# Latent attention of a decoder block on one Trainium2 core: instructions placed by a list scheduler written into the kernel, softmax reciprocals on VectorE, more low parts on GpSimd

## The chip, the cores and the metric

The kernel runs on one core of a Trainium2 chip. The time is device microseconds of that core, from several runs of the same program; the median is used. One further execution was taken with the hardware profiler. The engines are TensorE (PE; PEld is its weight load), VectorE (DVE), ScalarE (ACT), GpSimd (POOL) and SyncE (SP), which only issues transfers here. The built program has one queue of instructions for each engine, in a fixed order, with waits for the other engines' work.

## The reference

One layer of a decoder block on 1024 positions of width 1024, float32:

```
h = rmsnorm(x);  proj = h @ w_in  -> q, k, v of sliding-window attention, q_lat, kv_lat, k_rope, two gates
o_a = sliding-window attention (8 heads, window 128, sinks)
qb = rmsnorm(q_lat) @ w_uq  (8 heads x 96),  kvb = rmsnorm(kv_lat) @ w_ukv
for each 128-query block:  s = (q_nope k_nope + q_rope k_rope) * scale, causal
                           p = softmax(s);  o_b = p @ v
y = sigmoid(g_a) * (o_a @ w_o_swa) + sigmoid(g_b) * (o_b @ w_o_mla)
x = x + y @ w_out
x = x + (silu(rmsnorm(x) @ w_gate) * (rmsnorm(x) @ w_up)) @ w_down
out = rmsnorm(x)
```

The change concerns the latent attention (`o_b`): 8 heads, each with 8 blocks of 128 queries against up to 1024 keys.

## The kernel before

Products of float32 precision are made of three fast matmuls. Each operand is split into a high part (a rounded copy, made by ScalarE: a CAST at line 160) and a low part (the difference, a TENSOR_TENSOR at line 161, usually on VectorE), and `mm3` (lines 167 to 169) adds high x high, high x low and low x high in one PSUM bank.

The stages follow one another: projections, sliding-window attention with the gates' products, latent attention, output mixing (`mix_a`, `mix_b`), the product with `w_out`, the feed-forward part, the last norm.

In latent attention a step is one head h and one query block n, in the order n = 2, 3, 6, 7, 0, 1, 4, 5, so that a tile is (n + 1) x 128 keys wide: 384, 512, 896, 1024, 128, 256, 640, 768. For each step:

- `scores(t)`: PE makes the scores (tile `scb`, lines 1134 to 1136) in one of two score buffers; VectorE adds the mask and takes the row maximum (line 1144, with a read of its accumulator into `nmb`); ScalarE takes the exponential with the row sum (line 1145, tile `p`), after which the score buffer is free; GpSimd inverts the row sum `denb` by a power of -1 (line 1146) and scales `p` (line 1147).
- `transposes(t)`: PE turns `p` in groups of up to four 128x128 blocks (line 1161, tile `pTb`), ScalarE and VectorE split each group into `pth` and `ptl`.
- `pv(h, j)`: after every second block, PE multiplies with the values into the bank `ob` (lines 1183 and 1184); ScalarE copies one half to `otb` (line 1189) and VectorE adds it to the other (line 1195).

Between them stand the products that prepare the next heads: `prod_q` (tile `q`, then `qf` at line 1084, then `qT`, whose low part is on GpSimd) and `prod_k` (tile `k`, then `kT`), the splitting of their weights (`wr` to `wuq`), and in the last heads the splitting of the sliding-window outputs (`oar` to `wv`), of this attention's outputs (`ob` to `obT`), of the mixing weights (`wr` to `wh` and `wl`) and seven early `mix_a` products (tile `oA`). The tiles `pTb`, `ob`, `q`, `k` and the early `oA` share four PSUM banks.

The code writes the steps in a loop over t, with the scores two steps ahead and the other pieces tied to step numbers by tables (`OA_LOAD`, `OA_SPLIT`, `early`). The earlier stages set the order of some engines by hand (`tc.manual_schedule`), but this one does not: the framework orders every engine's queue here, starting from the order of the code.

Of the kernel before, what the change touches and what calls it, by code (L numbers as in the profile page):

```python
# [8 lines left out]
F32 = mybir.dt.float32  # L9
# [8 lines left out]
P = 128  # L18
# [33 lines left out]
class Stream:  # L52
# [30 lines left out]
    def get(self, key):  # L83
        i = self.index[key]
        self.conv_to(i)
        return self.done.pop(i)


@with_exitstack
def hybrid_block_kernel(  # L90
# [1023 lines left out]
    live = {}  # L1114
    pts = {}
    po_live = {}

    order = [2, 3, 6, 7, 0, 1, 4, 5]

    def step(t):  # L1120
        return t // NB, order[t % NB]

    def scores(t):
        h, n = step(t)
        w = (n + 1) * P
        sc = PX("scb", (P, 1024))
        qh, ql = qT[h]
        kh, kl = kT[h % 3]
        cw = 320 if w == 640 else 512
        for c0 in range(0, w, cw):  # L1130
            c1 = min(c0 + cw, w)
            kc = slice(c0, c1)
            o = slice(c0 // cw * 512, c0 // cw * 512 + c1 - c0)
            nc.tensor.matmul(sc[:, o], qh[:, blk(n)], kh[:, kc], start=True, stop=False)
            nc.tensor.matmul(sc[:, o], qh[:, blk(n)], kl[:, kc], start=False, stop=False)
            nc.tensor.matmul(sc[:, o], ql[:, blk(n)], kh[:, kc], start=False, stop=True)  # L1136
        nm = tiny("nmb")
        p = U("p")
        den = tiny("denb")
        s_, m_, p_ = sc[:, 0:w], mask[:, S - w:], p[:, 0:w]  # L1140
        if cw == 320:
            s_ = sc.rearrange("p (a c) -> p a c", a=2)[:, :, 0:320]
            m_, p_ = (v.rearrange("p (a c) -> p a c", a=2) for v in (m_, p_))
        nc.vector.tensor_tensor_reduce(s_, s_, m_, 1.0, -NEG, op0=ALU.add, op1=ALU.min, accum_out=nm)  # L1144
        nc.scalar.activation(p_, s_, AF.Exp, scale=-1.0, bias=nm, accum_out=den)  # L1145
        nc.gpsimd.tensor_tensor(den, den, neg_one[:, 0:1], op=ALU.pow)  # L1146
        nc.gpsimd.tensor_scalar(p[:, 0:w], p[:, 0:w], den, 0.0, op0=ALU.mult, op1=ALU.add)  # L1147
        live[t] = p

    def transposes(t):  # L1150
        h, n = step(t)
        p = live.pop(t)
        j, odd = divmod(n, 2)
        if not odd:
            pts[(h, j)] = [(U("pth", F32R, (P, 4, 256)), U("ptl", F32R, (P, 4, 256)))
                           for _ in range((2 * j + 5) // 4)]
        for k0 in range(0, n + 1, 4):
            m = min(4, n + 1 - k0)
            pp = P1("pTb", (P, 4, P))
            for i in range(m):  # L1160
                nc.tensor.transpose(pp[:, i], p[:, blk(k0 + i)], ident)  # L1161
            hi, lo = pts[(h, j)][k0 // 4]
            split(hi[:, 0:m, blk(odd)], lo[:, 0:m, blk(odd)], pp[:, 0:m])

    def pv(h, j):
        tiles = pts.pop((h, j))
        js = []
        for q in order:
            if q % 2:
                js.append(q // 2)  # L1170
        i = js.index(j)
        first = i % 2 == 0
        pair = sorted(js[i // 2 * 2:i // 2 * 2 + 2])
        slot = pair.index(j)
        if first:
            po_live[h] = P1("ob", (P, 2, 256))
        po = po_live[h][:, slot]
        nk = 2 * j + 2
        for kb in range(nk):
            q_off = P if kb == nk - 1 else 0  # L1180
            hi, lo = tiles[kb // 4]
            vst = vM[kb][:, h]
            nc.tensor.matmul(po[:, q_off:], vst, hi[:, kb % 4, q_off:], start=kb == 0, stop=False)
            nc.tensor.matmul(po[:, q_off:], vst, lo[:, kb % 4, q_off:], start=False, stop=kb == nk - 1)
        if not first:
            po = po_live[h]
            tmp = U("otb")
            tv = tmp[0:64, 0:512].rearrange("p (a c) -> p a c", a=2)
            nc.scalar.copy(tv, po[64:128])
            if h % 2 == 0 and i == 1:  # L1190
                ob[h // 2] = U("ob")
            r = (h % 2) * 64
            ov = ob[h // 2][r:r + 64].rearrange("p (a c) -> p a c", a=4)
            ov = ov[:, pair[0]:pair[1] + 1:pair[1] - pair[0]]
            nc.vector.tensor_tensor(ov, po[0:64], tv, op=ALU.add)

# [7 lines left out]

    def split_oa(g, sh, c):
        raw, (hi, lo) = oa_raw[(g, sh)] if c == 0 else oa_raw.pop((g, sh))
        split(hi[:, c], lo[:, c], raw[:, c])
        oaT[(2 * g + c, sh)] = (hi[:, c], lo[:, c])
# [12 lines left out]
    def mix_a(dc, sh, ps):  # L1221
        if sh == 0:
            if dc < 4:
                ar[dc] = U("ar")
            if dc % 2 == 0:
                wo[dc // 2] = st.get(("oa", dc // 2))
        w = wo[dc // 2]
        mm3(ps, [((w[0][:, c, blk(dc % 2)], w[1][:, c, blk(dc % 2)]), oaT[(c, sh)]) for c in range(4)])
        if dc < 4:
            nc.scalar.copy(ar[dc][:, half(sh)], ps)  # L1230
        else:
            ga = gate[dc][:, half(sh)]
            nc.vector.tensor_tensor(ga, ps, ga, op=ALU.mult)
# [5 lines left out]
    def split_ob(c, sh):  # L1239
        if sh == 0:  # L1240
            ob_hl[c] = hi_lo("obT")
        hi, lo = ob_hl[c]
        src = ob.pop(c) if sh else ob[c]
        split(hi[:, half(sh)], lo[:, half(sh)], src[:, half(sh)])
        obT[(c, sh)] = (hi[:, half(sh)], lo[:, half(sh)])

    wo = {}
    OA_LOAD = {-26: (0, 0), -22: (1, 0), -14: (0, 1), -10: (1, 1)}
    OA_SPLIT = {-22: (0, 0, 0), -20: (0, 0, 1), -18: (1, 0, 0), -16: (1, 0, 1),
                -10: (0, 1, 0), -8: (0, 1, 1), -6: (1, 1, 0), -4: (1, 1, 1)}  # L1250
    NT = NH * NB
    psum_phase("psb", 2)
    scores(0)
    scores(1)
    early = {0: (0, 0), 1: (1, 0), 3: (0, 1), 4: (1, 1), 5: (2, 0), 6: (2, 1), 7: (3, 0)}
    pvq = []
    for t in range(NT):
        h, n = divmod(t, NB)
        if t + 2 < NT:
            scores(t + 2)  # L1260
        while pvq and pvq[0][0] <= t:
            pv(*pvq.pop(0)[1:])
        if n == 0 and h % 2 == 0 and h + 2 < NH:
            st.load_to(st.index[("uq", h // 2 + 1)])
        if n == 0 and h % 2 == 1 and h + 1 < NH:
            wuq[(h + 1) // 2] = st.get(("uq", (h + 1) // 2))
        if h + 1 < NH:
            if n in (2, 4):
                prod_q(h + 1, n // 2 - 1)
            if n in (3, 5) and h % 2 == 1:  # L1270
                prod_k((h + 1) // 2, n // 2 - 1)
# [598 lines left out]
```

## Time and profile before

| what | value |
|---|---|
| median of the runs | 1364.37 us (1363.83 to 1364.56, 3 runs) |
| the profiled execution | 1360.19 us, its span 1358.4 us |
| busy, share of the span | PE 98%, DVE 70%, ACT 48%, POOL 44% |
| granted TensorE clock | 0.999 |
| latent attention | from 370 to about 568 us |

A span is the time from the first to the last instruction of the profile. Busy times are sums of instruction durations; those of PE are modelled at their ends. A row of the timeline gives the start, the duration, the engine, the line, the operation, the tiles as output<-input with shapes, and in brackets how long the engine had been idle before and what released it. A row of the waits gives the waiting engine, tile and line, what it waited for, the total in us, the number of times and the longest. Groups by line give total busy us and mean ns.

### The profile page before, as it was taken

Reading aid. Unit: us, or ns where it says so; the run is one execution under the profiler, and the core shown is the slowest. Engines: PE = TensorE matmul, PEld = TensorE weight load, DVE = VectorE, ACT = ScalarE, POOL = GpSimd, SP = SyncE. Lnnn points to the kernel's source line nnn. Section 1 sums busy time; section 2 is a strip of 40 time slices with the busy share of each in tenths; the row PEclk is TensorE's granted clock in tenths of the full one; section 3 lists DMA queues with packets and bytes.
Section 4 is the critical chain, followed back from the end, with each engine's and each line's share of the span. In section 5 each row is a group of like instructions: output and inputs, shape, how many; then the busy total and the mean of one; then the engine's idle time right before and its main releaser. Section 6 shows DMA issues by size and latency. Waiting matters only on the chain.

```text
span 1358.4 us, 18967 instructions
## 1 busy us (share of the span) xinstructions
PE 1331.8 (98%) x6552; PEld 1112.0 (82%) x6552; DVE 944.6 (70%) x1527; ACT 653.4 (48%) x1317; POOL 596.2 (44%) x636
## 2 busy tenths in 40 slices
PE   9999999999999999999999999999999999999997
PEld 6899878878788888888887788888888888888886
DVE  6868767776777887489878866666656664664862
ACT  7433667665567777654357232322332332644452
POOL 1115545553066555131045875766665541022521
PEclk9999999999999999999999999999999999999999
DMA  9454332335100111598041353645444425996503
GB/s 360 161 182 154 115 106 82 98 121 174 71 2 13 43 32 32 219 307 264 31 171 62 112 188 140 227 178 178 147 153 165 163 85 184 379 385 237 171 16 140
DMA packets 78239, 205.39 MB, mean 151 GB/s; under 512 B 8768, under 2 KB 15424, under 8 KB 77504
## 3 DMA queue, kind: packets, MB, share of 16 engines
q1 hardware_dynamic: 76848, 199.99, 41.5%
q0 software_dynamic: 1152, 4.19, 1.6%
q8 instruction: 52, 0.85, 0.3%
q14 instruction: 43, 0.35, 0.1%
q10 hardware_dynamic: 144, 0.00, 0.0%
HBM read 141.24 MB, written 59.77 MB: 148 GB/s over the span
## 4 chain that ended last, share of the span: by engine, by line
PE 72%; DVE 7%; ACT 4%; issue 3%; POOL 3%; DMA 0%; POOLq 0%; ACTq 0%; DVEq 0%
PE fa L169 7%; PE fa L167 7%; PE fa L168 7%; PE fd L168 5%; PE fd L167 5%; PE fd L169 5%; PE fb L167 5%; PE fb L169 5%; PE fb L168 5%; DVE wl L161 2%; PE pTb L1161 2%; PE xo L167 1%; PE xo L168 1%; PE xo L169 1%; PE oA L167 1%
## 5 line engine op out<-in xcount | busy, mean ns | idle before, releaser
L161 DVE TENSOR_TENSOR wl<-wr,wl 128x512 fp32r<-128x512 f32 x150 | 154.6, 1052 | 75.4 <-ACT wl L160 75.1
L161 DVE TENSOR_TENSOR lrv<-lr,lrv 128x1024 fp32r<-128x1024 f32 x77 | 105.0, 1396 | 49.7 <-ACT lrv L160 47.1
L160 ACT CAST lrv<-lr 128x1024 fp32r<-128x1024 f32 x77 | 80.1, 1052 | 96.3 <-PE fd L169 56.0
L169 PE MATMUL fd<-lrv 128*128 128x512 f32 x308 | 119.9, 389 | 0.0
L168 PE MATMUL fd<-lrv 128*128 128x512 f32 x308 | 119.9, 389 | 0.0
L167 PE MATMUL fd<-lrv 128*128 128x512 f32 x308 | 119.9, 389 | 0.0
L172 POOL TENSOR_TENSOR wr<-wr,sm 128x512 f32<-128x512 f32 (+1 forms) x38 | 46.8, 1241 | 121.2 <-DVE wl L161 115.1
L160 ACT CAST wl<-wr 128x512 fp32r<-128x512 f32 x150 | 87.3, 623 | 3.1 <-DVE wr L816 2.6
L161 DVE TENSOR_TENSOR wl<-sm,wl 128x512 fp32r<-128x512 f32 x60 | 55.2, 946 | 45.4 <-ACT wl L160 45.4
L295 POOL TENSOR_SCALAR ms<-ss 128x1 f32<-128x1 f32 x32 | 9.8, 305 | 140.4 <-ACT xn L1582 62.5
L1146 POOL TENSOR_TENSOR denb<-denb,neg_one 128x1 f32<-128x1 f32 x64 | 36.4, 570 | 75.0 <-ACT p L1145 64.3
L167 PEld LDWEIGHTS fd<-lrv 128*128 128x128 f32 x308 | 57.8, 188 | 12.1
L169 PEld LDWEIGHTS fd<-lrv 128*128 128x128 f32 x308 | 57.8, 188 | 12.0
L168 PEld LDWEIGHTS fd<-lrv 128*128 128x128 f32 x308 | 57.8, 188 | 11.9
L1145 ACT ACTIVATE p<-scb,nmb 128x384 f32<-128x384 f32 (+3 forms) x64 | 47.5, 743 | 36.8 <-DVE nmb L1144 35.0
L161 DVE TENSOR_TENSOR ptl<-pTb,pth 128x512 fp32r<-128x512 f32 (+2 forms) x96 | 50.0, 549 | 13.6 <-ACT pth L160 12.8
L1144 DVE CUSTOM_DVE_ANT_0 scb<-scb,mask 128x384 f32<-128x384 f32 (+3 forms) x64 | 48.5, 758 | 14.1 <-PE scb L1136 13.7
L1485 ACT ACTIVATE act<-sm 128x512 f32<-128x512 f32 x11 | 7.0, 633 | 103.7 <-DVE sm L175 103.7
L1147 POOL TENSOR_SCALAR p<-p,denb 128x384 f32<-128x384 f32 (+3 forms) x64 | 49.1, 768 | 6.3
L1485 ACT ACTIVATE act<-pu 128x512 f32<-128x512 f32 x22 | 13.9, 632 | 74.8 <-DVE pu L175 74.8
L160 ACT CAST pth<-pTb 128x512 fp32r<-128x512 f32 (+2 forms) x96 | 42.9, 482 | 13.5 <-PE pTb L1161 12.9
L169 PE MATMUL fa<-t1h,wl 128*128 128x512 f32 x120 | 46.8, 391 | 2.6 <-DVE wl L161 2.6
(354 smaller groups left out, 4374.8 us busy)
## 6 DMA issues: line engine op xcount, KB each, us to landing
lr<-la_d SPq DMA_DIRECT2D x77, 256.0 KB, 5.4
wr<-in_w_gate_dram SPq DMA_DIRECT2D x22, 512.0 KB, 4.3
wr<-in_w_up_dram SPq DMA_DIRECT2D x22, 512.0 KB, 5.0
wd<-in_w_down_dram SPq DMA_DIRECT2D x22, 512.0 KB, 6.4
rb_d<-wd SPq DMA_DIRECT2D x22, 512.0 KB, 2.6
la_d<-sd SPq DMA_DIRECT2D x22, 512.0 KB, 4.8
lr<-rb_d SPq DMA_DIRECT2D x44, 256.0 KB, 5.4
lr<-in_w_down_dram SPq DMA_DIRECT2D x33, 256.0 KB, 5.6
```

The lines of the kernel that those rows point to most:

```text
L160: nc.scalar.copy(hi, src)
L161: (eng or nc.vector).tensor_tensor(lo, src, hi.bitcast(F32), op=ALU.subtract)
L167: nc.tensor.matmul(ps, ah, bh, start=first and i == 0, stop=False, skip_group_check=go_on)
L168: nc.tensor.matmul(ps, ah, bl, start=False, stop=False, skip_group_check=go_on)
L169: nc.tensor.matmul(ps, al, bh, start=False, stop=last and i == n - 1, skip_group_check=go_on)
L172: eng.tensor_tensor(out, a, b, op=ALU.subtract)
L1144: nc.vector.tensor_tensor_reduce(s_, s_, m_, 1.0, -NEG, op0=ALU.add, op1=ALU.min, accum_out=nm)
L1145: nc.scalar.activation(p_, s_, AF.Exp, scale=-1.0, bias=nm, accum_out=den)
L1146: nc.gpsimd.tensor_tensor(den, den, neg_one[:, 0:1], op=ALU.pow)
L1147: nc.gpsimd.tensor_scalar(p[:, 0:w], p[:, 0:w], den, 0.0, op0=ALU.mult, op1=ALU.add)
L1161: nc.tensor.transpose(pp[:, i], p[:, blk(k0 + i)], ident)
L1485: nc.scalar.activation(dst, src, AF.Silu)
```

## The change

The loop over steps is taken out. Each piece of work becomes a step of a `Plan` with an engine, an assumed duration in ns, the steps that it comes after, a rank, and the PSUM buffer that it takes or gives back: S (scores), M (maximum), E (exponential), W (reciprocal), C (scaling), T, H, L (transposes, high and low part), V, O, A (values, copy, sum), Q and K with their splits, u, o, w and b (splits of weights and outputs), G (early mixing products). `Plan.run` builds the order with a clock of its own: for each engine it takes, among the steps that could start within 30 ns of the earliest one, the step of lowest rank (its place in the sequence plus a constant for its kind), and issues the engine's earliest choice. PE, DVE, ACT and POOL then keep exactly this order in the stage; SP is left to the framework.

Two things change in what is computed where. The reciprocal of the row sum is a VectorE reciprocal in place of a GpSimd power. And the low parts of `wuq`, `wv` (from `oar`), `obT` and the four mixing weights converted here are made by GpSimd in place of VectorE; `qT` was there before. All 64 steps, all matmuls and all transfers remain; the splits of the last output block, which stood behind the loop, come into the plan, and so does the eighth early mixing product.

```diff
+    TAIL = {"E": 0, "D": 80, "A": 100, "P": 36, "S": 0}
+    HOP = {"E": 70, "D": 36, "A": 36, "P": 79, "S": 50}
+
...
+    def add(self, name, eng, cost, emit, after=(), rank=0.0, take=None, give=None, port=False, group=None):
+        self.steps[name] = (eng, cost, emit, list(after), rank, take, give, port, group)
+
...
+                for name in names:
+                    _, _, _, _, rank, take, _, _, group = steps[name]
+                    t = max(free[eng], since[name])
+                    if take is not None:
+                        s = slots[take[0]]
+                        if group in rows:
+                            if rows[group][turn[group]] != name:
+                                continue
+                            s = [s[turn[group] % len(s)]]
+                        if take[2] and sum(x < busy for x in s) <= take[2]:
+                            continue
+                        t = max(t, min(s) + self.HOP[eng])
+                    if t < busy:
+                        can.append((t, rank, name))
+                if can:
+                    t0 = min(can)[0]
+                    t, rank, name = min((c for c in can if c[0] <= t0 + self.slack), key=lambda c: (c[1], c[2]))
+                    if best is None or t < best[0]:
+                        best = (t, name)
+            t, name = best
+            eng, cost, emit, _, _, take, give, two, group = steps[name]
+            ready[eng].remove(name)
+            if eng == "P" or two:
+                t = max(t, port)
+                port = max(port, t + (100 if eng == "P" and not two else cost - 140))
+            end[name] = t + cost + (160 if eng == "E" else 0)
+            free[eng] = t + cost - self.TAIL[eng]
...
-        nc.vector.tensor_tensor_reduce(s_, s_, m_, 1.0, -NEG, op0=ALU.add, op1=ALU.min, accum_out=nm)
-        nc.scalar.activation(p_, s_, AF.Exp, scale=-1.0, bias=nm, accum_out=den)
-        nc.gpsimd.tensor_tensor(den, den, neg_one[:, 0:1], op=ALU.pow)
-        nc.gpsimd.tensor_scalar(p[:, 0:w], p[:, 0:w], den, 0.0, op0=ALU.mult, op1=ALU.add)
...
-        hh, nn = step(t)
-        if nn % 2 == 1:
-            pvq.append((t + 3, hh, nn // 2))
-        e = t - (NT - 8)
-        if e in OA_LOAD:
-            load_oa(*OA_LOAD[e])
-        if e in OA_SPLIT:
-            split_oa(*OA_SPLIT[e])
-        if e == -5:
-            st.conv_to(st.index[("oa", 0)])
-        if -3 <= e < 3:
-            split_ob((e + 3) // 2, (e + 3) % 2)
-        if e == 6:
-            psum_phase("psc", 4)
-        if e == 7:
-            st.conv_to(st.index[("ob", 0)])
-        if e in early:
-            mix_a(*early[e], (PX if e >= 6 else P1)("oA"))
-        if e == 4:
-            st.conv_to(st.index[("oa", 1)])
...
+    plan = Plan(30)
+    RANK = {'S': -2.38, 'M': -0.6, 'E': -2.86, 'W': -2, 'C': -2, 'V': 3.5, 'O': 1.49, 'A': 2.32, 'Q': -0.9, 'Qm': 2.11, 'Qh': 1.76, 'Ql': 0.5, 'K': -0.3, 'Kh': 0.92, 'Kl': 0.91, 'uh': -1.71, 'ul': -0.83, 'wl': 6.31, 'G': 2.93, 'wh': 0.76, 'bl': 0.9, 'ol': -0.89, 'H': -0.5, 'oh': -0.63}
+    LOW = {'Q': 'P', 'u': 'P', 'o': 'P', 'b': 'P', 'w': 'P'}
...
+        def maxes():
+            t_["p", key] = U("p")
+            nm = t_["nm", key] = tiny("nmb")
+            s_, m_, _ = views(t_["p", key])
+            nc.vector.tensor_tensor_reduce(s_, s_, m_, 1.0, -NEG, op0=ALU.add, op1=ALU.min, accum_out=nm)
+
+        def exps():
+            den = t_["den", key] = tiny("denb")
+            s_, _, p_ = views(t_["p", key])
+            nc.scalar.activation(p_, s_, AF.Exp, scale=-1.0, bias=t_.pop(("nm", key)), accum_out=den)
+            t_.pop(("sc", key))
+
+        def invert():
+            den = t_["den", key]
+            nc.vector.reciprocal(den, den)
+
+        def scale():
+            p, den = t_["p", key], t_.pop(("den", key))
+            nc.gpsimd.tensor_scalar(p[:, 0:w], p[:, 0:w], den, 0.0, op0=ALU.mult, op1=ALU.add)
+
...
+        add_step("M", *key, x=x, eng="D", emit=maxes, cost=210 + 1.055 * w, after=[("S", *key)])
+        add_step("E", *key, x=x, eng="A", emit=exps, cost=350 + 0.836 * w, after=[("M", *key)], give=("sc", key))
+        add_step("W", *key, x=x, eng="D", emit=invert, cost=100, after=[("E", *key)])
+        add_step("C", *key, x=x, eng="P", emit=scale, cost=232 + 0.878 * w, after=[("W", *key)], port=True)
...
+    def lower(kind, key, x, cost, hi, lo, src, after=()):
+        add_step(kind + "h", *key, x=x, eng="A", emit=lambda: nc.scalar.copy(hi(), src()), cost=cost[0], after=after)
+        on_p = LOW[kind] == "P"
+        add_step(kind + "l", *key, x=x, eng="P" if on_p else "D", port=True, cost=cost[1 + on_p], after=[(kind + "h", *key)],
+                 emit=lambda: sub(lo(), src(), hi().bitcast(F32), nc.gpsimd if on_p else nc.vector))
...
+        add_step("Q", h, s, x=x, eng="E", emit=prod, cost=2060, take=("p", ("q", h, s), 1),
+                 after=[("ul", h // 2, 0), ("ul", h // 2, 1), ("S", h - 2, NB - 1)])
+        add_step("Qm", h, s, x=x, eng="D", emit=rope, cost=683, after=[("Q", h, s)], give=("q", h, s))
+        lower("Q", (h, s), x, (621, 692, 1290), lambda: part(0), lambda: part(1), lambda: t_["qf", h, s],
+              [("Qm", h, s), ("S", h - 2, NB - 1)])
...
+    by_plan = tc.manual_schedule(engines={engines.PE, engines.DVE, engines.Activation, engines.Pool})
+    by_plan.__enter__()
+    plan.run({"x": 2, "p": 4, "w": 4}, {"S": [("S", h, i) for h in range(NH) for i in range(NB)]})
+    by_plan.__exit__(None, None, None)
...
-    split_ob(3, 0)
-    split_ob(3, 1)
+    ob.clear()
```

The order of the built programs differs at these places. The first is PE at the start of the stage, at the scores (`scb`) of the second tile and what follows. Before:

```order
L1134 MATMUL scb_4179<-kT_3994,qT_4037 128x512
L1135 MATMUL scb_4179<-kT_3994,qT_4037 128x512
L1136 MATMUL scb_4179<-kT_3994,qT_4037 128x512
L1134 MATMUL scb_4190<-kT_3994,qT_4037 128x512
L1135 MATMUL scb_4190<-kT_3994,qT_4037 128x512
L1136 MATMUL scb_4190<-kT_3994,qT_4037 128x512
L1134 MATMUL scb_4190<-kT_3994,qT_4037 128x384
```

Now:

```order
L1270 MATMUL scb_4174<-kT_3994,qT_4037 128x512
L1271 MATMUL scb_4174<-kT_3994,qT_4037 128x512
L1272 MATMUL scb_4174<-kT_3994,qT_4037 128x512
L256 MATMUL q_4183<-cq_3810,wuq_3916 128x512
L257 MATMUL q_4183<-cq_3810,wuq_3916 128x512
L258 MATMUL q_4183<-cq_3810,wuq_3916 128x512
L256 MATMUL q_4183<-cq_3811,wuq_3916 128x512
```

The third tile's scores (`scb_4190` before) now come nine matmuls later, behind a product `q` for the next head. The second place is ACT towards the end of head 6, at the exponential of the 640-wide tile. Before:

```order
L1145 ACTIVATE p_5966,denb_5967<-scb_5961,nmb_5965 128x256
L160 CAST pth_5946<-pTb_5985 128x4x128
L160 CAST wv_5809<-oar_5808 128x512
L160 CAST obT_6051<-ob_4394 128x512 x2
L160 CAST obT_6118<-ob_4947 128x512 x2
L160 CAST wh_5974<-wr_5972 128x1024
L160 CAST obT_6191<-ob_5510 128x512
L1145 ACTIVATE p_6000,denb_6001<-scb_5992,nmb_5999 128x640
L160 CAST obT_6191<-ob_5510 128x512
```

Now:

```order
L1290 ACTIVATE p_5984,denb_5988<-scb_5961,nmb_5985 128x256
L1326 CAST pth_5958<-pTb_5990 128x4x128
L1326 CAST pth_5976<-pTb_5997 128x4x128
L1376 CAST qT_5941<-qf_5995 128x512
L1326 CAST pth_6027<-pTb_6015 128x128
L1290 ACTIVATE p_6032,denb_6042<-scb_6004,nmb_6033 128x640
L1326 CAST pth_6027<-pTb_6044 128x2x128
L1290 ACTIVATE p_6047,denb_6069<-scb_6035,nmb_6048 128x768
L1357 COPY otb_6077<-ob_6018 64x512
L1326 CAST pth_6094<-pTb_6080 128x4x128
L1290 ACTIVATE p_6085,denb_6099<-scb_6072,nmb_6086 128x384
L1376 CAST obT_6112<-ob_4407 128x512
```

The conversions of `obT` and of the mixing weight `wh` stood in a row ahead of that exponential; now they stand later, one or two at a time between exponentials. The third place is POOL in head 4, at the scaling of the 1024-, 128- and 256-wide tiles. Before:

```order
L1146 TENSOR_TENSOR denb_5317<-denb_5317,neg_one 128x1
L1147 TENSOR_SCALAR p_5316<-p_5316,denb_5317 128x1024
L1146 TENSOR_TENSOR denb_5335<-denb_5335,neg_one 128x1
L1147 TENSOR_SCALAR p_5334<-p_5334,denb_5335 128x128
L161 TENSOR_TENSOR qT_5355<-qf_5366,qT_5355 128x512
L1146 TENSOR_TENSOR denb_5398<-denb_5398,neg_one 128x1
L1147 TENSOR_SCALAR p_5397<-p_5397,denb_5398 128x256
```

Now, from the 512-wide tile on:

```order
L1299 TENSOR_SCALAR p_5279<-p_5279,denb_5284 128x512
L261 TENSOR_TENSOR wv_5334<-oar_5197,wv_5334 128x512
L1299 TENSOR_SCALAR p_5300<-p_5300,denb_5312 128x896
L1299 TENSOR_SCALAR p_5319<-p_5319,denb_5339 128x1024
L1299 TENSOR_SCALAR p_5362<-p_5362,denb_5368 128x128
L261 TENSOR_TENSOR qT_5365<-qf_5347,qT_5365 128x512
L261 TENSOR_TENSOR wv_5334<-oar_5197,wv_5334 128x512
L1299 TENSOR_SCALAR p_5415<-p_5415,denb_5419 128x256
```

The powers are gone from this queue, and low parts of `wv` stand between scalings. The reciprocals stand in DVE's queue, as here in the same head:

```order
L1295 RECIPROCAL denb_5284<-denb_5284 128x1
L1285 ISA scb_5272,nmb_5301<-scb_5272,mask_4034 128x896
L1285 ISA nmb_5301 128x1
L261 TENSOR_TENSOR ptl_5297<-pTb_5286,pth_5296 128x3x128
L1285 ISA scb_5304,nmb_5320<-scb_5304,mask_4034 128x1024
L1285 ISA nmb_5320 128x1
L1295 RECIPROCAL denb_5312<-denb_5312 128x1
L261 TENSOR_TENSOR ptl_5297<-pTb_5314,pth_5296 128x4x128
L1390 TENSOR_TENSOR qf_5347<-q_5324,rope_t_3967 128x512
```

Each reciprocal waits for the exponential of its tile, with the next maximum or low part behind it.

More of the change, by code (lines that the diff above doesn't have):

```diff
@@ L1150, in transposes @@
[L1150 to L1195, printed above, removed]
@@ new lines, in weight_steps, with load, part @@
+    def weight_steps(j):
+        x = NB * (2 * j - 1)
+        def load():
+            t_["uq", j] = st.take(("uq", j))
+            wuq[j] = {}
+        add_step("u0", j, x=x - 8, eng="S", cost=400, emit=load, after=[("S", 2 * j - 2, 0), ("ul", j - 1, 1)])
+        for u in range(2):
+            def part(i, u=u):
+                if u not in wuq[j]:
+                    wuq[j][u] = U("wuq", F32R, (P, 2, 3, P))
+                return wuq[j][u][:, i]
+            lower("u", (j, u), x, (500, 920, 1890), lambda part=part: part(0), lambda part=part: part(1),
+                  lambda u=u: t_["uq", j][:, u], [("u0", j), ("S", 2 * j - 2, 6)])
```

318 lines of the change are left out of this document (246 added, 72 removed).

## Prediction

> **What bounds the kernel now.** I read first the busy times on the page, then the busy time by stage, then the stretches in which TensorE stood still.
>
> ```profile
> PE 1331.8 (98%) x6552; PEld 1112.0 (82%) x6552; DVE 944.6 (70%) x1527; ACT 653.4 (48%) x1317; POOL 596.2 (44%) x636
> 370.00:470.00 100.00, 97.28 (x614) 84.39 (x613) 75.44 (x159) 69.42 (x161) 59.93 (x83) 1.00 0.06 20
> 470.00:568.00 98.00, 93.59 (x561) 80.39 (x560) 69.49 (x136) 66.28 (x145) 43.32 (x59) 1.00 0.17 59
> 568.00:640.00 72.00, 72.00 (x319) 59.66 (x318) 60.25 (x79) 35.92 (x42) 17.33 (x12) 1.00 0.96 311
> ```
>
> TensorE sets the end. The change touches the stage from about 370 to 568 us alone (latent attention). The columns after the window are its length, then busy time of PE, PEld, DVE, ACT and POOL, the granted clock, the DMA share and GB/s. PE is idle there for 2.72 + 4.41 = 7.1 us, at full clock, with the DMA engines nearly idle. From 568 us on it is never idle. The change adds and removes no matmul. So its gain can only be time in which PE now waits in this stage, and that is small.
>
> Busy ends of PE are modelled, so I also measure by starts.
>
> ```profile
> 516.38 0.39 PE L168 MATMUL q<-cq,wuq 128*128 128x512 f32 x1
> 516.61 0.39 PE L169 MATMUL q<-cq,wuq 128*128 128x512 f32 x1
> 371.69 0.40 PE L1136 MATMUL scb<-kT,qT 128*128 128x512 f32 x1
> 372.87 0.50 PE L1134 MATMUL scb<-kT,qT 128*128 128x512 f32 x1 [0.78 <-ACT p L1145]
> 560.03 0.28 PE L1184 MATMUL ob<-ptl,vM 128*128 128x128 f32 x1
> 560.35 0.39 PE L1183 MATMUL ob<-pth,vM 128*128 128x256 f32 x1
> ```
>
> A 512-column matmul is shown as 0.39 but the next starts 0.23 later. A wait shown as 0.78 idle therefore costs 1.18 - 0.23 = 0.95. Counted like that, 21 places in the stage start more than 0.15 late, the first at 371.69 and the last at 560.03 (0.26 late), together 10.85 us. The idle column gives 7.1; with 21 x (0.39 - 0.23) added it is 10.5, so the two agree. **The most that perfect ordering can win is 10.85 us.** The Trainium skill (Perfetto Trace Analysis, Tensor Engine Instruction) says that a matmul's end is computed by the profiler and not observed; by a reader who takes the ends at their word the ceiling would be 7.1, and the rows just shown (0.39 long, 0.23 apart) side with the page.
>
> **Where the 10.85 us lie.** Five groups, by what PE waited for.
>
> ```profile
> PE k L167 <- DVE ob L1195: 2.2, 3, 0.8
> PE pTb L1161 <- POOL p L1147: 1.8, 4, 0.7
> PE q L167 <- DVE ptl L161: 0.7, 2, 0.4
> 522.77 0.77 PE L1161 MATMUL pTb<-ident,p 128*128 128x128 f32 x5 [0.68 <-POOL p L1147]
> 524.27 0.50 PE L1134 MATMUL scb<-kT,qT 128*128 128x512 f32 x1 [0.73 <-ACT p L1145]
> 526.03 0.66 PE L1161 MATMUL pTb<-ident,p 128*128 128x128 f32 x4 [0.56 <-POOL p L1147]
> 517.78 0.13 DVE L1144 DVE_READ_ACCUMULATOR2_ANT nmb<- 128x1 f32 x1
> 516.24 2.21 ACT L160 CAST obT<-ob 128x512 fp32r<-128x512 f32 x4
> 518.33 1.07 ACT L160 CAST wh<-wr 128x1024 fp32r<-128x1024 f32 x1
> 519.29 0.63 ACT L160 CAST obT<-ob 128x512 fp32r<-128x512 f32 x1
> 519.80 0.81 ACT L1145 ACTIVATE p<-scb,nmb 128x640 f32<-128x640 f32 x1
> ```
>
> 1. The first three waits (371 to 381 us), 1.70: scores wait for the only two score buffers.
> 2. k after ob, three times, 2.69: the product of keys waits until the value product's PSUM bank is emptied.
> 3. q after ptl, twice, 1.13: a bank again.
> 4. 522 to 526 us, 2.52. The row maximum of the 640-wide tile is done at 517.91, but ScalarE is in a row of six conversions (four of obT, one of wh, one of obT) that nobody needs yet and starts the exponential at 519.80. The scaling on GpSimd, the transposes and the next scores are late one after the other.
> 5. Four waits from 500 to 506 us, 1.37, and the scattered rest, 1.44.
>
> **The change, part by part.**
>
> *Order.* (1) Between the scores of the second and third tile there now stand the nine matmuls of a q product, 9 x 0.23 = 2.1 us; the wait there was 1.18 from start to start. Gone: 1.70. (2) In the new order the first k matmul waits for the DVE product that reads the q product before it, which PE finished 2.6 us of its own work earlier; that reader is one 128x512 operation. Gone: 2.69. (3) Half gone: 0.56. (4) In the new ScalarE order no exponential of these heads stands behind more than one or two such conversions, of 0.6 to 1.1; I leave 0.5 of it, 2.02 gone. (5) Group 5 half gone where it is clustered (0.7), the scattered rest I leave as it is, since something of that sort will return elsewhere.
>
> I checked the order for new tight places by one sum for each tile: PE's own work between a tile's scores and the point that needs its exponential (or its transposes), against the chain that must fit in.
>
> ```profile
> L1144 DVE CUSTOM_DVE_ANT_0 scb<-scb,mask 128x896 f32<-128x896 f32 x8 | 8.7, 1090 | 1.3 <-PE scb L1136 1.3
> L1144 DVE DVE_READ_ACCUMULATOR2_ANT nmb<- 128x1 f32 x64 | 8.9, 139 | 0.0
> L1145 ACT ACTIVATE p<-scb,nmb 128x896 f32<-128x896 f32 x8 | 8.1, 1009 | 9.5 <-DVE nmb L1144 9.5
> L1145 ACT ACTIVATION_READ_ACCUMULATOR p<-scb,nmb 128x1 f32 x64 | 12.5, 196 | 0.0
> L1147 POOL TENSOR_SCALAR p<-p,denb 128x896 f32<-128x896 f32 x8 | 8.9, 1110 | 0.8
> L1146 POOL TENSOR_TENSOR denb<-denb,neg_one 128x1 f32<-128x1 f32 x64 | 36.4, 570 | 75.0 <-ACT p L1145 64.3 <-PE pTb L1161 10.5
> ```
>
> For the 896-wide tile of head 2 the chain to the exponential's end is 1.09 + 0.14 + 1.01 + 0.20 = 2.44, and 0.17 for the last matmul's tail. Until the scores that reuse its buffer PE had 2.73 us of work, margin 0.12; now q's 2.04 stands there too and the margin is 1.92. Over all tiles and both needs (128 places), 22 had a margin under 0.6 before and 8 have now; none is negative now, nine were. That leaves some small waits: I charge 0.8 for new ones.
>
> *Reciprocal.* GpSimd loses 64 powers of 0.57, 36.4 us. DVE gets 64 reciprocals of one column, which this trace doesn't show; nearest are these.
>
> ```profile
> L338 DVE MEMSET neg_half<- 128x1 f32 x1 | 0.1, 59 | 0.8 <-PEq L1848 0.8
> L905 DVE SCALAR_TENSOR_TENSOR nm<-mx,nsink 128x4 f32<-128x4 f32 x16 | 2.8, 177 | 0.5
> L161 POOL TENSOR_TENSOR qT<-qf,qT 128x512 fp32r<-128x512 f32 x14 | 18.5, 1321 | 7.9 <-ACT qT L160 7.9
> L1304 POOL TENSOR_TENSOR sg<-ar,sg 128x1024 f32<-128x1024 f32 x4 | 10.4, 2612 | 22.3 <-ACT sg L1217 22.3
> L161 DVE TENSOR_TENSOR wuq<-wr,wuq 128x384 fp32r<-128x384 f32 x6 | 5.3, 918 | 0.0
> L161 DVE TENSOR_TENSOR wv<-oar,wv 128x512 fp32r<-128x512 f32 x8 | 7.9, 1009 | 0.0
> L161 DVE TENSOR_TENSOR obT<-ob,obT 128x512 fp32r<-128x512 f32 x8 | 5.2, 692 | 1.5 <-ACT obT L160 1.5
> L161 DVE TENSOR_TENSOR wl<-wr,wh 128x1024 fp32r<-128x1024 f32 x4 | 4.8, 1219 | 0.2 <-ACT wh L160 0.2
> ```
>
> Bounds 0.06 and 0.18; I take 0.15 (it computes, like the second), 9.6 us in all. The chain from exponential to transposes is 0.4 shorter for each tile; that is in the margins above.
>
> *Low parts.* 26 subtractions go from DVE to GpSimd: 6 of wuq, 8 of wv, 8 of obT, 4 of wl. DVE loses 5.3 + 7.9 + 5.2 + 4.8 = 23 us. GpSimd gets 16 x 1.32 + 4 x 2.61 + 6 x (0.99 to 1.32, by size or by the whole 512 row) = 37 to 40. So DVE goes from 145 busy to about 131 of 198 us and GpSimd stays near 103 to 107. Neither becomes the bound, and what hides these parts is PE's own work; uncovered, one costs the difference between its length and the margin of the tile behind it, 0.7 us at a margin of 0.6.
>
> *Behind the stage.* The loads of the gates wait for buffers that the attention frees, in the new order after an earlier matmul than before; PE has work there in any case (third windows row). No gain and no loss.
>
> **Sum.** Gone 1.70 + 2.69 + 0.56 + 2.02 + 0.7 = 7.67, less 0.8 for new waits: 6.9 us. The profiled execution took 1360.19 (span 1358.4 and 1.8 around it), 4.2 under the median of the runs; on it the sum gives 1353.3, on the median 1364.37 - 6.9 = **1357.5 us**.
>
> **Rivals.**
>
> *A. The wait moves to DVE (no change).* Before, GpSimd alone stood and waited for the exponential (75.0 us of idle in the row of the power). Now DVE does, and in it the next maximum, the low parts and the q product queue behind. Working through DVE's new order with the rows above, at 28 of 64 reciprocals there is less DVE work since that tile's maximum than its exponential takes, 14.9 us in all. If PE pays half, 7.5, the gain is gone: 1365. Against it: DVE idles 53 of 198 us in the stage, so most of this takes the place of idle time.
>
> *B. GpSimd is late (slower).* A low part of 1.3 or 2.6 that has just begun holds up the scaling of the next tile, for which the transposes wait. If this bites at 16 of the wide-enough places (0.7 each) and at the four 1024-wide ones (2.0 each) it is 19 lost: 1364.4 - 6.9 + 19 = 1377; half of it, 1367. It decides against the change from about ten late scalings on. The Trainium skill (GPSIMD Engine Reference, Engine selection) advises VectorE for elementwise work on a tile and puts GpSimd at about twice the time with two inputs; the rows above agree (1.32 against 0.69 to 1.01). For it: the new order puts such parts directly ahead of a scaling. Against: those scalings have margins of 1 to 4 us by the sum above.
>
> *C. All 21 waits go:* 1364.4 - 10.85 = 1353.5. For it: all margins are positive. Against: they ignore queues.
>
> *D. The list order is in effect the old one.* PE still runs two score tiles ahead in nearly the same sequence, and in heads 2 to 6 many rows stand as they did; if only the first group and the conversions of group 4 change, 3.7 gained, less 0.8 for new waits, it is 1361.5.
>
> **How the numbers follow.** Forecast 0.58 (own range 1354.5 to 1360.5), A 0.13, B 0.09, C 0.11, D 0.09. What can be told from no change is 0.2%, 2.7 us: faster is below 1361.6, slower above 1367.1. Faster: forecast, C and half of D, 0.58 + 0.11 + 0.05 = 0.74. Same: A and the other half of D, 0.17. Slower: B, 0.09. The range reaches down to C, 1353.0, and up over A to 1365.0; outside lie B and a little of A and C.
>
> **What would show it.** Right: PE idle between 370 us and the stage's end falls from 7.1 to about 2.5; no row of k waiting for ob; no exponential of head 6 more than about 0.7 after its maximum; the stage ends near 561. A: rows of DVE in which the reciprocal or what follows it waits for ACT, and PE waits for DVE. B: PE waiting for POOL's p by more than the 1.8 us that the stage shows now. I would be wrong altogether if the 568 to 640 stretch or the start of the feed-forward part shows PE idle that isn't there now.

## The result and the profile after

The changed kernel takes 1346.93 us, median of 4 runs (1346.85 to 1347.89); the kernel before took 1364.1 in the same set of runs (1361.94 to 1364.56). The ratio is 0.9896, 95% interval 0.988 to 0.9912. A later set of runs gave 0.9902 (0.9879 to 0.9925), with 1347.22 against 1360.82. The predicted 1357.5 is 10.6 us too slow, and the result lies below the range.

Busy times on the page after, and then busy time by stretch (length, then PE, PEld, DVE, ACT, POOL, granted clock, DMA share, GB/s). The first stretch runs from the first score matmul to the first `oB` matmul, which I call the stage from here on; the second follows it.

```profile
PE 1325.4 (99%) x6552; PEld 1112.4 (83%) x6552; DVE 927.2 (69%) x1565; ACT 653.5 (49%) x1317; POOL 591.5 (44%) x598
369.17:556.33 187.16, 186.89 (x1179) 166.45 (x1178) 130.11 (x333) 138.45 (x306) 102.53 (x105) 1.00 0.18 60
556.00:628.00 72.00, 72.00 (x320) 59.60 (x319) 61.20 (x82) 34.12 (x41) 15.84 (x12) 1.00 0.91 275
```

The same stretch before:

```profile
370.70:570.22 199.52, 192.39 (x1180) 166.06 (x1178) 145.09 (x295) 137.79 (x305) 103.47 (x143) 1.00 0.13 43
```

The stage is 12.36 us shorter. The profiled executions differ by 13.2 us (1360.19 and 1347.01); the rest is a start 1.53 earlier, ahead of anything that the change touches, and some 0.7 given back behind `xo`, where the granted clock of the execution after is 0.50 for 3.41 us from 743.10 and that of the execution before never is. PE's idle time fell from 7.1 to 0.27 us. But the stage lost 12.4, and PE's *busy* time for the same matmuls fell too, from 192.4 to 186.9: the other half of the loss had been counted as work.

The waits of the stage after. PE itself has no row left; these are its weight load's and, below, the two largest of what the change added.

```profile
PEld pTb L1315 <- DVE ob L1365: 0.6, 2, 0.3
PEld scb L1270 <- ACT p L1290: 0.5, 2, 0.2
PEld pTb L1315 <- issue: 0.4, 2, 0.2
PEld q L256 <- DVE ob L1365: 0.2, 1, 0.2
DVE denb L1295 <- ACT p L1290: 14.2, 19, 1.2
POOL p L1299 <- DVE denb L1295: 52.3, 31, 13.0
```

VectorE now stands before 19 reciprocals for 14.2 us, and no wait of PE's own comes of it. The groups of the moved work (total us, mean ns, then idle time before them):

```profile
L1295 DVE RECIPROCAL denb<-denb 128x1 f32<-128x1 f32 x64 | 10.1, 158 | 14.7 <-ACT p L1290 14.2
L261 POOL TENSOR_TENSOR obT<-ob,obT 128x512 fp32r<-128x512 f32 x8 | 10.2, 1292 | 11.3 <-ACT obT L1376 11.3
L261 POOL TENSOR_TENSOR wl<-wr,wh 128x1024 fp32r<-128x1024 f32 x4 | 9.6, 2401 | 2.3 <-PE ob L1353 1.1 <-ACT wh L1376 0.8 <-POOL p L1299 0.3
L261 POOL TENSOR_TENSOR wuq<-wr,wuq 128x384 fp32r<-128x384 f32 x6 | 6.1, 1023 | 0.0
```

And the exponential of the 640-wide tile of head 6, which had waited from 517.91 to 519.80 behind six conversions; in the timeline after, its maximum ends at 508.21 and it starts at 508.30:

```profile
508.07 0.14 DVE L1285 DVE_READ_ACCUMULATOR2_ANT nmb<- 128x1 f32 x1
508.30 0.79 ACT L1290 ACTIVATE p<-scb,nmb 128x640 f32<-128x640 f32 x1 [1.24 <-POOL qT L261]
```

### The profile page after: what moved, and what is told of

It is laid out like the page before. It is cut to its first block, busy times and chain, and to the rows that moved or that the text cites. A ratio compares the mean times of both kernels' runs of the same rounds, so it can differ in the third digit from the quotient of the medians.

```text
span 1345.2 us, 18917 instructions
## 1 busy us (share of the span) xinstructions
PE 1325.4 (99%) x6552; PEld 1112.4 (83%) x6552; DVE 927.2 (69%) x1565; ACT 653.5 (49%) x1317; POOL 591.5 (44%) x598
## 5 line engine op out<-in xcount | busy, mean ns | idle before, releaser
L256 PEld LDWEIGHTS fd<-lrv 128*128 128x128 f32 x308 | 57.8, 188 | 12.1
L258 PE MATMUL fa<-t1h,wl 128*128 128x512 f32 x120 | 47.4, 397 | 2.6 <-DVE wl L250 2.6
L258 PE MATMUL fb<-t3h,wl 128*128 128x512 f32 x120 | 47.2, 394 | 1.7 <-DVE wl L250 1.7
L256 PE MATMUL fa<-t1h,wl 128*128 128x512 f32 x120 | 47.9, 399 | 0.0
## 6 DMA issues: line engine op xcount, KB each, us to landing
wr<-in_w_gate_dram SPq DMA_DIRECT2D x22, 512.0 KB, 4.3
wr<-in_w_up_dram SPq DMA_DIRECT2D x22, 512.0 KB, 5.3
wd<-in_w_down_dram SPq DMA_DIRECT2D x22, 512.0 KB, 6.8
rb_d<-wd SPq DMA_DIRECT2D x22, 512.0 KB, 2.6
la_d<-sd SPq DMA_DIRECT2D x22, 512.0 KB, 5.4
```

The costliest lines, as they stand in the source:

```text
L256: nc.tensor.matmul(ps, ah, bh, start=first and i == 0, stop=False, skip_group_check=go_on)
L258: nc.tensor.matmul(ps, al, bh, start=False, stop=last and i == n - 1, skip_group_check=go_on)
```

## The experiments

The stage's length is the finest measure here: two executions of the kernel before gave 199.51 and 199.56 us, two of the changed kernel 187.16 and 187.09, while whole runs of the kernel before spread over 7.6 us. Of the other versions one execution each was profiled. All times of runs are medians; where there was one run, that is said.

| order | reciprocal | low parts | stage us | run us | ratio to before (95%) |
|---|---|---|---|---|---|
| framework (before) | GpSimd | VectorE | 199.5 | 1360.1 to 1364.1, by set | 1 |
| framework | VectorE | VectorE | 196.9 | 1358.55 | 0.9977 (0.9963 to 0.9992) |
| framework | GpSimd | GpSimd | 208.3 | 1366.95 | 1.0044 (1.003 to 1.0057) |
| framework | VectorE | GpSimd | 202.8 | 1364.01 | 1.0017 (1.0004 to 1.0031) |
| framework | VectorE | `wuq`, `wv` on GpSimd, rest VectorE | 195.5 | 1355.16 | 0.9948 (0.9931 to 0.9964) |
| list | GpSimd | VectorE | 191.1 | 1350.99 | 0.9929 (0.9915 to 0.9944) |
| list | VectorE | VectorE | 190.4 | 1350.46 | 0.9923 (0.9908 to 0.9939) |
| list | GpSimd | GpSimd | 190.2 | 1350.12 | 0.992 (0.9906 to 0.9935) |
| list (the change) | VectorE | GpSimd | 187.1 | 1347.22 | 0.9902 (0.9879 to 0.9925) |
| list, no ranks | VectorE | GpSimd | 199.2 | 1358.96 | 0.9978 (0.9965 to 0.9992) |
| list, five ranks | VectorE | GpSimd | 192.4 | 1352.49, one run | |
| list, seven other ranks | VectorE | GpSimd | 199.2 | 1358.82, one run | |
| PE alone, new order | | | 185.4 | 1345.77, one run | |
| PE alone, old order | | | 185.3 | 1345.07, one run | |

### The two kernels again

The kernel before, without an edit:

> The kernel before, unchanged, for a second profile. The medians of before and after differ by 17.2 us, the two profiled executions by 13.2. Theory 1 (the profiled execution of before was a lucky one, and in its others the latent attention stage is as long, but something later is longer): this execution takes 1362 to 1364.5 with the stage at 199.5 us from the first score to the first oB product, and the 2 to 4 us more lie behind 640 us, where the gates' and feed-forward loads run. Theory 2 (the stage itself varies): the stage is 202 to 204 here.

Its stage was 199.56 us, so theory 2 falls; but the median of 12 runs was 1360.13 (1358.39 to 1362.57), below what theory 1 said. The first profile, at 1360.19, lies at that level; the three runs shown with it lay high in the spread. In the two profiles the stage starts at 370.70 and 369.13, and from the first `xo` matmul to the first `fd` one it is 511.2 and 512.0. So these two executions differ outside the stage, ahead of it and in the feed-forward part. The second difference goes with the granted clock: it is 0.50 for 3.41 us from 753.87 in the second execution and stays at 1.00 there in the first. Over all 16 profiles this stretch is 511.1 to 511.2 us where the clock stays up (three), 512.0 to 512.3 with one such interval (twelve) and 513.6 with one of 6.83 us.

> The changed kernel, unchanged, on the same chip as the next three and beside more runs of the kernel before, since the kernel before took 1364.1 in one set of runs and 1361.5 in the next. Expected 1346.5 to 1348, the stage 187.2 us from the first score to the first oB product.

1347.22 (1346.34 to 1348.46), stage 187.09.

### What TensorE alone needs

In both orders the matmuls stay and the work between the scores and the values goes: maximum, exponential, reciprocal, scaling and the splits of the transposes, so that the outputs are not those of the layer (three of the edits, for the new kernel):

```diff
-                nc.tensor.transpose(pp[:, k], t_["p", key][:, blk(4 * g + k)], ident)
+                nc.tensor.transpose(pp[:, k], p0[:, blk(4 * g + k)], ident)
...
-            tiles = t_.pop(("pt", h, j))
+            tiles = [hl0, hl0]
...
-        add_step("E", *key, x=x, eng="A", emit=exps, cost=350 + 0.836 * w, after=[("M", *key)], give=("sc", key))
+        add_step("E", *key, x=x, eng="A", emit=lambda: None, cost=350 + 0.836 * w, after=[("M", *key)], give=("sc", key))
```

> The floor of TensorE in the new order. Every matmul of the stage stands where it stood, but maximum, exponential, reciprocal, scaling and the splits of the transposes are left out; the transposes read the constant mask and the value products a constant pair of tiles, so PE waits for none of them. (The output of the latent attention is therefore not the reference's.) Theory W (all that the stage lost to others is waiting, in pieces too small to have been counted one by one): the stage is 184 to 186 us here, and the same in the old order. Theory T (the order of the matmuls has a price of its own, by what stands next to what): the new order's floor is 2 us or more below the old one's.

> The same in the kernel before: the same parts of the computation left out, the old order of TensorE but for 66 of its rows. Theory W: within 0.7 us of the new order's floor, so that before the change 14 to 15 us, not 10.85, were to be won. Theory T: 2 us or more above the new order's floor.

The stage in busy time by stretch, first the new order:

```profile
369.71:555.09 185.38, 185.38 (x1179) 166.48 (x1178) 30.40 (x45) 49.73 (x82) 54.99 (x41) 1.00 0.19 63
```

and the old one:

```profile
369.12:554.43 185.31, 185.31 (x1179) 166.29 (x1178) 49.82 (x71) 49.63 (x82) 19.60 (x15) 1.00 0.17 55
```

Theory W holds: the floor is 185.3 to 185.4 us in either order, with no idle time at all. (In the old order's run the framework placed 66 of PE's rows otherwise.) Before the change the stage was 14.2 us above it, after the change 1.8. So neither order of the matmuls shows a price of its own; what it changes is what they wait for.

Set beside the floor matmul by matmul (where both have the same sequence, which holds 12.6 of the 14.2 us), the old kernel has 19 places more than 0.15 us late, 9.9 us together, and some 40 places between 0.02 and 0.15 late, 2.4 us. The remaining 1.6 lie where the floor's order differs from the old one. After the change six places are more than 0.15 late, the longest 0.27.

The Trainium skill (Perfetto Trace Analysis, Tensor Engine Instruction) says that a matmul's end is computed and not observed. The runs agree, and show what it does to a sum: the same 1179 or 1180 matmuls are 185.3 us busy alone, 186.9 after and 192.4 before. Only 7.1 of the 14.2 us of waiting stood in the idle column.

### The order without the moved work, and each part in the list

The list's rows are kept and only the engine of an instruction goes back:

```diff
-            nc.vector.reciprocal(den, den)
+            nc.gpsimd.tensor_tensor(den, den, neg_one[:, 0:1], op=ALU.pow)
...
-                 emit=lambda: sub(lo(), src(), hi().bitcast(F32), nc.gpsimd if on_p else nc.vector))
+                 emit=lambda: sub(lo(), src(), hi().bitcast(F32), nc.gpsimd if kind == "Q" else nc.vector))
```

The first alone, the second alone, both:

> The changed kernel with its list order kept, but the 64 reciprocals back on GpSimd as powers (0.57 each). Theory O (the order carries the gain): the chain of each tile is 0.4 longer, which the margins mostly cover: 1347.5 to 1350. Theory P (the shorter chain carries it): 1353 or more, with PE waiting for POOL's p at 10 or more places.

> The changed kernel with its list order kept, but the 26 low parts of wuq, wv, obT and wl back on VectorE. VectorE gets 23 us more in the stage, GpSimd 37 to 40 less. Theory O: 1347 to 1349. Theory P: GpSimd's and VectorE's instructions with two SBUF inputs slow each other again (0.92 to 1.0 instead of 0.69 on VectorE) and hold up the maxima behind them: 1351 or more.

> The changed kernel's order alone: powers on GpSimd and the 26 low parts on VectorE, as before the change, in the places that the list gives them. Theory O (order carries the gain): 1348 to 1352, at least 12 of the 17.2 us. Theory P (the moved work carries it): 1357 or more.

Stages of 190.2, 190.4 and 191.1. The third run, 1350.99, lies where theory O put it; the first two, 1350.12 and 1350.46, lie between the theories. The order alone is worth 8.4 of the 12.4 us, and the moved work 4.0 on top. This order was planned for the moved work; a list planned for the old division of the work was not tried. The two parts don't add: undoing either costs 3.0 to 3.3, undoing both 4.0. In the waits of the run with powers on GpSimd, PE stands before POOL's scaling again:

```profile
PE pTb L1315 <- POOL p L1299: 1.5, 4, 0.4
PEld pTb L1315 <- POOL p L1299: 4.5, 12, 0.7
```

and with the low parts on VectorE the next scores stand before exponentials:

```profile
PE scb L1270 <- ACT p L1290: 1.0, 3, 0.6
PEld scb L1270 <- ACT p L1290: 2.0, 5, 0.7
```

### The moved work without the list

The kernel before with `nc.vector.reciprocal(den, den)` at line 1146 and the four splits given `nc.gpsimd`; the framework orders as it did.

```diff
-        nc.gpsimd.tensor_tensor(den, den, neg_one[:, 0:1], op=ALU.pow)
+        nc.vector.reciprocal(den, den)
...
-        split(hi[:, half(sh)], lo[:, half(sh)], src[:, half(sh)])
+        split(hi[:, half(sh)], lo[:, half(sh)], src[:, half(sh)], nc.gpsimd)
```

> The kernel before with both engine changes and without the list: the reciprocal on VectorE and the 26 low parts on GpSimd, the order left to the framework. With the order alone the stage went from 199.5 to 191.1 us, so the parts gave 4.0 in the new order. Theory O (parts help only where the order is good, because the old waits are for conversions and banks): 1358 to 1361, stage 197 to 199. Theory P (the parts give their 4 anywhere): stage 195.5, 1357.5. Rival A of the prediction (VectorE stands before the reciprocal): stage above 199.5.

202.76 us, slower than before by 3.2: only rival A's number fits, and for another reason. GpSimd's timeline, with the end of ScalarE's exponential among it and the matmul that waits at its end:

```profile
510.99 1.30 POOL L161 TENSOR_TENSOR wv<-oar,wv 128x512 fp32r<-128x512 f32 x1
512.24 5.04 POOL L161 TENSOR_TENSOR obT<-ob,obT 128x512 fp32r<-128x512 f32 x4
514.90 0.22 ACT L1145 ACTIVATION_READ_ACCUMULATOR p<-scb,nmb 128x1 f32 x1
517.23 2.36 POOL L161 TENSOR_TENSOR wl<-wr,wh 128x1024 fp32r<-128x1024 f32 x1
519.52 1.28 POOL L161 TENSOR_TENSOR obT<-ob,obT 128x512 fp32r<-128x512 f32 x1
520.74 1.28 POOL L161 TENSOR_TENSOR qT<-qf,qT 128x512 fp32r<-128x512 f32 x1
521.98 1.70 POOL L1147 TENSOR_SCALAR p<-p,denb 128x640 f32<-128x640 f32 x2
522.86 1.33 PE L1161 MATMUL pTb<-ident,p 128*128 128x128 f32 x5 [6.36 <-POOL p L1147]
```

The exponential of the 640-wide tile is done at 515.12, but its scaling starts at 521.98: eight low parts stand in a row ahead of it, the burst of group 4, now on a slower engine, and five of them are not done when the exponential is. PE stands still for 6.4 us. And the wait costs more than its length, as the windows before and after 527.04 show (the columns are those of the stage above):

```profile
522.86:527.04 4.18, 4.18 (x15) 3.59 (x16) 1.54 (x4) 1.27 (x3) 2.62 (x3) 0.50 0.00 0
527.04:531.22 4.18, 4.18 (x24) 3.56 (x23) 2.79 (x7) 1.76 (x5) 0.69 (x1) 1.00 0.00 0
```

From 520.21 to 527.04 the granted clock is 0.50, and the first 15 matmuls behind the stall lose another 1.9 us against the same matmuls in the floor. This is rival B, at a single place, and at 8.4 us instead of the 0.7 to 2.0 that the prediction gave one place. Elsewhere the stage is better than before: no row of k waiting for `ob` is left, though no product was moved ahead of it.

> The kernel before with the reciprocal alone moved to VectorE, the order left to the framework. Both engine changes together made the stage 202.75 us there (199.5 before), with one stall of 6.5 us at 523 us, where TensorE waits for a scaling behind nine low parts in GpSimd's queue. Theory Q (that queue is what the parts cost): no such stall here, and the chain 0.4 shorter for each tile: stage 197 to 199. Theory A (VectorE, standing before reciprocals, holds up maxima): stage 199.5 to 202.

Theory Q: 196.9, no such stall. But 2.45 of the 2.6 us won were given back in the next stretch (from the first `oB` to the first `xo`, 62.29 us; 59.84 in the kernels before and after), where PE waits once for a low part on VectorE:

```profile
PE oB L169 <- DVE wl L161: 2.1, 1, 2.1
```

> The kernel before with the 26 low parts alone moved to GpSimd, the powers left there too, the order left to the framework. Theory Q: the same stall at about 523 us, longer by the powers in the queue, 6.5 to 8 us; the rest of the stage as before or better, since VectorE has 23 us less and k no longer waits for it: stage 202 to 206. Theory A: 199 to 200, no stall, as the cost was the reciprocal's.

Longer than either theory, 208.3: the stall of 6.4 is there, three further places of the same wait add 3.7, and PE also waits for low parts themselves. The powers of 0.55 remain in the same queue. The granted clock is 0.50 here too, for 3.41 us behind a wait of 2.4 and for 6.83 us in and behind the stall, which makes up some 3.9 of the 8.8 us.

```profile
PE pTb L1161 <- POOL p L1147: 10.1, 4, 6.4
PE scb L1134 <- ACT p L1145: 1.2, 2, 0.8
PE oA L169 <- POOL wl L161: 1.1, 1, 1.1
PE q L169 <- POOL wuq L161: 0.9, 2, 0.5
```

> The kernel before with the reciprocal on VectorE and the low parts of wuq and wv on GpSimd, but those of obT and wl left on VectorE; the order left to the framework. Theory Q: the six low parts of obT and wl that stood in GpSimd's queue ahead of one scaling are gone, and with them 6 us: stage 195.5 to 197.5. Otherwise 200 or more.

195.5 and no long stall, as theory Q said. So the same moves are worth 4.0 us without the last-head low parts, and cost 3.2 with them, 1.9 of it by the clock, both in the framework's order (PE's sequence differs from the old one at 8 and 10 of 1179 places); in the list's order, where those parts stand one or two at a time between scalings, they can all be moved.

### The rank table

The changed kernel with one of these three in place of its table:

```diff
+    RANK = {}
...
+    RANK = {'S': -2.38, 'M': -0.6, 'E': -2.86, 'W': -2, 'C': -2}
...
+    RANK = {'V': 3.5, 'O': 1.49, 'A': 2.32, 'Q': -0.9, 'K': -0.3, 'G': 2.93, 'wl': 6.31}
```

> The changed kernel with its table of ranks emptied, so that among steps that can start within 30 ns of each other the plan takes the earliest in the sequence of tiles, whatever its kind. 624 of TensorE's rows differ from the changed kernel's. Theory R (the constants matter): waits of TensorE in the stage rise from 1.8 to 5 us or more, stage 190.5 or more. Theory L (listing by readiness is enough): 186.5 to 189.

> The changed kernel with a rank table of five entries, which puts scores, maximum, exponential, reciprocal and scaling some two places of the sequence ahead of everything else; all other constants are gone. With the empty table the stage was 199.2 us, with the full one 187.1. Theory C (what counts is that nothing stands ahead of the chain of a tile): stage 187.5 to 190. Theory F (what counts is that TensorE's fill work, values and products, is held back for the places where it would wait): 194 or more, since the values here stand where the empty table has them.

> The changed kernel with a rank table of the other kind: value products, their copy and sum, mixing products and their low parts held back, q and k as in the full table, and no constant for scores, maximum, exponential, reciprocal and scaling. Theory C: 194 or more, since conversions and splits stand ahead of exponentials again. Theory F: 187.5 to 190.

Theory R holds: with an empty table the kernel gains nothing in the stage (199.2; 199.5 before). Beside the framework's order with the same work moved (202.8) the bare list is still 3.6 us better. Its largest row of waits:

```profile
PE scb L1271 <- ACT p L1291: 5.6, 7, 1.2
```

With only the five entries that put a tile's chain first the stage is 192.4, 6.8 of the 12.1 us between empty and full; the same row reads

```profile
PE scb L1270 <- ACT p L1290: 1.8, 4, 0.7
```

The seven entries for fill work alone gave no gain (199.25), in an execution in which a wait of 1.85 us was followed by 3.41 us at a granted clock of 0.50; at full clock it would have been up to 1.7 us shorter. Neither theory's numbers were met in full: the chain first is a condition, and the other constants bring the last 5.3 us only on top of it. Which of them do was not tried.

## Why the prediction was wrong

The direction, the stage and the mechanism were right. The miss of 10.6 us has three terms, and a remainder of 0.9 outside the stage.

**The ceiling: 3.35 us.** The step that failed is "The most that perfect ordering can win is 10.85 us". The floor shows 14.2. The sum was made of places more than 0.15 us late, and the check against the idle column only counted the same places again, corrected for the same modelled ends. Some 40 smaller delays, of 0.02 to 0.15 each, lay under the threshold; they are 2.4 of the 3.35, and the other 0.9 is not traced to places. Rival C, "all 21 waits go", was the right mechanism with that ceiling.

**What was kept: 2.1 us.** The sum kept 3.95 us of waiting (half of group 3, 0.5 of group 4, half of group 5's cluster, the scattered rest, and 0.8 new). 1.8 is left. The margins, of which none was negative any more, said so; I did not trust them and wrote "something of that sort will return elsewhere" without a row for it.

**The base: 4.2 us.** The sum on the profiled execution gave 1353.3, and I moved it to "the median 1364.37", of three runs. Later sets gave medians of 1360.1 to 1362.2 for the same kernel, near the profiled execution. The changed kernel's runs lie within 2.1 us, those before within 7.6 (1357.87 to 1365.47). Part of the spread goes with the granted clock: in the largest set, runs above 1363 us have a mean granted clock of 0.996 to 0.998 and those below 1360 of 0.998 to 0.999, which is worth about 2 of the 5 us between the two groups. The rest is open.

Point by point, the rest:

- *Two slips without effect.* By the terms given for the 896-wide tile the new margin is 0.12 + 2.04 = 2.16, not 1.92. Of the 75.0 us of idle time in the row of the power, 64.3 were for the exponential and 10.5 for PE's transposes.
- *Groups.* All five are gone. For group 2 the reason given, that the bank is freed by the reader of q, is not needed: in the old order the moved reciprocal alone removes these waits too, with four of PE's rows changed. For group 4 it holds: the exponential starts 0.09 after its maximum.
- *Reciprocal.* Estimated 0.15, measured 0.158. *Low parts*: estimated 1.32, 2.61 and 0.99 to 1.32, measured 1.29, 2.40 and 1.02. VectorE's busy time in the stage was put at 131 and is 130.1; GpSimd's at 103 to 107 and is 102.5.
- *"What hides these parts is PE's own work"* is true of the list's order alone. Their worth depends on it: +3.2 us in the old order, -4.0 in the new.
- *Rival A.* The waits before reciprocals came as worked out (14.2 us at 19 places; 14.9 at 28 in the prediction), and took the place of idle time, as the argument against it said.
- *Rival B* did not happen here because the list spreads the low parts. Where they stood in a row it did, with a wait of 6.4 us and 1.9 us lost to the halved clock behind it, at one place.
- *Rival D* did not happen, and no run tests it: with an empty rank table the list gives the old time, but not the old order (in 875 of the stage's 1179 places PE has a matmul of another tile or shape than before).
- *What would show it.* No row of k waiting for `ob`, no late exponential in head 6, no idle time behind the stage: right. Idle 0.27 instead of "about 2.5", and the stage's end 5 us before "561": the ceiling again, but for the 1.5 us by which the stage starts earlier.

No version tried that computes the whole layer beats the changed kernel. In this stage 1.8 us, 0.13% of the time, are left above PE's floor.

## What to carry to other kernels

Find the bounding engine's floor by leaving its partners out, not by adding up its visible waits: half of the waiting here stood in its busy time, and a sixth lay in pieces too small to list. Work moved to a slower engine is priced by what stands behind it in that engine's queue at the worst place; the same move was worth 4 us in one order and cost 3 in another, the more so as a long wait was followed by a slower clock. A list scheduler is as good as its priorities: with none, the changed kernel took the old time.

## What the runs showed of the hardware

I had not expected how much VectorE and GpSimd slow each other. Before the change, beside one another (VectorE's two `wv` low parts, then GpSimd's `qT` and power):

```profile
497.56 2.42 DVE L161 TENSOR_TENSOR wv<-oar,wv 128x512 fp32r<-128x512 f32 x2
497.70 1.72 POOL L161 TENSOR_TENSOR qT<-qf,qT 128x512 fp32r<-128x512 f32 x1
499.39 0.99 POOL L1146 TENSOR_TENSOR denb<-denb,neg_one 128x1 f32<-128x1 f32 x1
```

In the list's order with the low parts on VectorE, the same eight subtractions have these times:

```profile
L261 DVE TENSOR_TENSOR wv<-oar,wv 128x512 fp32r<-128x512 f32 x8 | 5.5, 684 | 0.0
```

So one takes 0.68 us undisturbed and 1.01 on average before. In the merged row above the first takes 0.72 and the second, beside `qT`, 1.78; GpSimd's 1.30 became 1.72, and a power of 0.55 became 0.99. The list's clock counts such pairs as exclusive and places them apart. The Trainium skill (SBUF — State Buffer, Who interferes with whom) says that a VectorE instruction with two SBUF inputs contends with a GpSimd instruction that reads SBUF; these rows agree. Part of what the low parts win on GpSimd may be that; no run separates it from the shorter VectorE queue.

The second thing is the clock. In all 16 profiles, from the first record of it (4 to 10 us) to the last matmul, the granted clock is 1.00 but for intervals of 3.41 or 6.83 us at 0.50. Each of these begins in a wait of PE of 1.85 us or more, or within 1.6 us behind it: the four in the stage with waits of 6.4 (twice), 2.4 and 1.85 us, and 13 with a wait of 2.6 us that every version has in the feed-forward part. No wait of up to 1.6 us is followed by one. Not every long wait is: in three profiles the one of 2.6 us is not, nor is the one of 2.1 us behind the stage in the run with the reciprocal alone moved. Before the change the longest wait of the stage was 0.78 us, so this was no part of what the change won.
